# A hybrid decoder layer on one core: the sums of the output weights by accumulating transfers, and the value sums of an attention block in one run

## The chip, the cores and the metric

The kernel runs on one core of a Trainium2 chip. The metric is device time in microseconds of one execution, as the median of several runs. The core has five engines that run side by side, each with an instruction queue worked off in order: TensorE (PE; its weight loads are the row PEld), VectorE (DVE), ScalarE (ACT), GpSimd (POOL) and SyncE (SP), which here only issues transfers. Transfers issued by SP are listed under queue q1, those issued by POOL under q0; both run on the same 16 DMA engines.

## The reference, cut to what matters

One layer is computed for a prompt of 2048 tokens and for 32 sample tokens with a paged cache. A projection `z = rms_norm(x) @ w_in` is split into four groups (convolution, pooling, stick-breaking attention, attention into a memory), each group is gated, and the concatenation goes through `w_out`:

```python
def sb_block(q, k, v, bias, q_pos, k_pos):          # 8 heads of 64, causal
    z = q.k * dh**-0.5 + bias
    log_1m = where(mask, log_sigmoid(-z), 0)
    rc = cumsum(log_1m, reverse=True)               # along the keys
    a = exp(where(mask, log_sigmoid(z) + rc - log_1m, -inf))
    return a @ v
...
mix = concatenate([y_c * silu(cg), y_p * silu(pg), y_s * silu(sg), y_m * silu(mg)])   # 2048 wide
out = rms_norm(mix @ w_out, post_g)                 # w_out: 2048 x 1024
y = rms_norm(x + out, final_g)
```

## The kernel before

The program has three stages. First the input projections, beside them the sample group with its cache, whose pages POOL fetches by indirect transfers (0 to about 1475 us). Then the attention of the prompt (about 1485 to 1922 us). Then the output projection with `w_out`, beside it the end of the convolution group (about 1922 us to the end).

**The attention** (`sb_prompt`) runs over 16 blocks (hp, qb): four pairs of heads, and in each four groups of 512 queries. A block goes over its groups of keys kc from qb down to 0, so qb + 1 of them; over all blocks there are 40 (block, kc) pairs. One such pair is four steps (`score`), one for each head hh of the pair and each half q2 of the queries. A step issues four score products on PE (L1297, L1298: S), on ACT the sigmoids of S (L1302: gam, L1303: be; for some steps DVE forms gam as 1 - be, L1363), two steps later on DVE two scans (L1372 in the diagonal pair, L1375 otherwise: E), and on POOL the multiplication be * E (L1384). Four steps after the score (`TURN`) `turn` puts the 128x128 pieces of be through PE transposes (L1403: AT, two PSUM buffers) and ACT copies them to SBUF (L1405: at, `ATB` buffers). `values` multiplies the turned pieces with V (L1415: av, one PSUM buffer, the two heads side by side in two halves of 64 columns of the array); it is called once for each half q2. When a block's last pair is done, DVE multiplies av by its gate (L1419: sgt, one buffer), SP stores it to `mixd` and then loads the next gate (L1436).

`late` is the list of these delayed calls: each has the step at which it is due, and `behind(step)` issues what is due, after that step's score. A pair that starts at step `base` has its transposes at base + 4, 5, 6 and 7, and its value sums at base + 7 and base + 9.

**Side work** (`side_work`) is a generator, stepped about once for every 4 us of estimated attention time. In this order it runs the end of the sample group, `weight_sums`, the first product's weights (`out_weights(1, ...)`: casts on ACT, low parts on POOL, L1668), the first four operands of the output projection, and the start of `conv_post`.

**The output projection** multiplies 2x2 blocks with seven products instead of eight. Four of them take sums of blocks of `w_out` as weights. `weight_sums` makes those sums: for each of eight row tiles SP loads two tiles of 128x1024 (L1620), POOL forms four differences or sums of 128x512 in SBUF (L1627), and SP stores two tiles to the DRAM tensor `wsd` (L1630). They are read back in the output projection (L1641, L1653). `FACTORS` and `SUMS` say which product uses which.

The order of PE's instructions is the order of the code. On the other engines and on the queues a list scheduler places instructions by its own estimates, within the data dependencies; `tc.issue_after(x)` adds that the instruction stands behind x. Tiles of one tag share the number of buffers given as `bufs`.

Of the kernel before, what the change touches and what calls it, by code (L numbers as in the profile page):

```python
# [18 lines left out]
P = 128  # L19
# [46 lines left out]
SUM = 3  # L66
BEB = 5
ATB = 6
# [24 lines left out]
def kernel(  # L93
# [1227 lines left out]
    def sb_prompt(load, loaded, sb, bps, ops, zmp, early, values_of, flags, newest):  # L1321
# [108 lines left out]
        for bi, (hp, qb) in enumerate(blocks):  # L1430
# [5 lines left out]
            sp.dma_start(gt, gsd[hp, :, 512 * qb : 512 * qb + 512])  # L1436
            carry = {}
            for kc in range(qb, -1, -1):
                base = step
                for q2 in (0, 2):  # L1440
                    for hh in range(2):
                        cost = 1.33 * (2 * q2 + 3) / 4 if kc == qb else 2.66
                        rest = score(hp, qb, kc, hh, q2, Q, KT, carry)
                        if len(pend) == 2:
                            pend.pop(0)()
                        pend.append(rest)
                        yield cost / 2
                        behind(step)
                        step += 1
                        yield cost / 2  # L1450
                for n, q2 in ((0, 0), (2, 2)):
                    late.append((base + n + TURN + SUM, lambda a=(hp, qb, kc, q2, V, gt): values(*a)))
                    for hh in range(2):
                        late.append((base + n + hh + TURN, lambda a=(hp, qb, kc, hh, q2): turn(*a)))
                late.sort(key=lambda x: x[0])
# [9 lines left out]
    def conv_post(cp, ps_, weights):  # L1465
# [61 lines left out]
        def gate(i, co):  # L1527
            a0, a1 = blocks[i]
            gates[i, co] = cp.tile([P, CW], F32, tag="cgt", name=f"cgt{a0}_{co}", bufs=3)
            wq.dma_start(gates[i, co][:, : a1 - a0], gcd[co, :, a0:a1])  # L1530
# [82 lines left out]
    def weight_sums(wsp):  # L1613

        ts = {}
        for j in range(9):
            if j < 8:
                ts[j] = [wsp.tile([P, 2, 512], F32, tag="ws", name=f"ws{j}_{n}", bufs=6) for n in range(2)]
                for t, r in zip(ts[j], half_rows(j)[::-1]):
                    sp.dma_start(t.rearrange("p b n -> p (b n)"), w_out0[r])  # L1620
            yield
            if j:
                t, u = ts.pop(j - 1)
                for o, a, b, op_ in ((t[:, 1], t[:, 1], u[:, 1], ALU.subtract), (u[:, 1], u[:, 1], u[:, 0], ALU.subtract),
                                     (u[:, 0], t[:, 1], u[:, 0], ALU.add), (t[:, 0], t[:, 0], u[:, 0], ALU.subtract)):
                    with tc.issue_after(newest[-1]):
                        pool.tensor_tensor(out=o, in0=a, in1=b, op=op_)  # L1627
                    yield
                for n, o in enumerate((t, u)):
                    sp.dma_start(wsd[n, j - 1], o)  # L1630
                yield

# [103 lines left out]
    def out_combine(x):  # L1736
# [3 lines left out]
        if prod == 5 and i < LAST:  # L1740
            dve.tensor_tensor(out=ts[1], in0=ts[0], in1=ts[1], op=ALU.add)
# [4 lines left out]
        elif prod == 6:  # L1746
            tc.keep_in_program_order(dve.tensor_tensor(out=ts[0], in0=ts[0], in1=ts[1], op=ALU.subtract))
# [25 lines left out]
    def out_ready(prod, i, o):  # L1773

        if i == LAST:
# [12 lines left out]
            else:  # L1788
                dve.tensor_tensor(out=o[:NS], in0=both[:NS], in1=keep["s"][:NS], op=ALU.add)
# [11 lines left out]
        elif prod == 6:  # L1801
            dve.tensor_tensor(out=U3[:, i], in0=o, in1=U3[:, i], op=ALU.add)
            dve.tensor_tensor(out=U2[:, i], in0=o, in1=U2[:, i], op=ALU.add)
# [5 lines left out]
        else:  # L1809
# [9 lines left out]
            dve.tensor_tensor(out=c, in0=o, in1=(U2 if prod == 3 else U3)[:, i], op=ALU.add)  # L1819
# [152 lines left out]
    flags, W, newest = set(), {}, []  # L1972
# [17 lines left out]
    def side_work():  # L1990
# [3 lines left out]
        with tc.tile_pool(name="wsp", bufs=1, side="left", reuse_waits="tile") as wsp:  # L1994
            yield from weight_sums(wsp)
# [217 lines left out]
```

## Time and profile before

| | |
|---|---|
| median of 3 runs | 2313.46 us (2313.35 to 2315.27) |
| the profiled execution | 2319.3 us, of it span of instructions 2317.6 us |
| granted clock of TensorE, mean | 0.993 |
| PE, PEld busy | 2244.9 us (97%), 1812.9 us (78%) |
| DVE, ACT, POOL busy | 1704.7 us (74%), 1081.0 us (47%), 1261.0 us (54%) |
| weight sums (L1627) | 32 instructions on POOL, from 1550.0 to 1762.5 us |
| transfers of the weight sums | 16 loads and 16 stores of 512 KB on SP |

Shares over the whole span are means over three stages that have different limits. What bounds the attention is read from stretches of it: the busy time of each engine in such a stretch, and the granted clock there (1.00 is the upper level of 2.4 GHz, 0.5 is 1.2 GHz). The ends of pipelined matmuls are modelled, so the busy time of PE is read with the distances from start to start in the timeline.

### The profile page before, as it was taken

What the parts mean: (1) busy time and instruction counts of PE and PEld (TensorE: products, weight loads), DVE (VectorE), ACT (ScalarE), POOL (GpSimd) and SP (SyncE); (2) the same over time, 40 slices, a digit from 0 to 9 for tenths busy, and PEclk for the clock granted to TensorE, in tenths of its full rate; (3) what the DMA queues carried; (4) which work ended last, traced back from release to release, by engine and by line L of the source; (5) the groups of instructions that cost most, each with busy time, mean ns of one, the idle gap of its engine ahead of it and who ended that gap; (6) DMA issues with size and microseconds to landing.
All of it is one profiled execution on the core that took longest, in us unless ns stands there. A gap on an engine that the chain in (4) does not pass through costs nothing. (4 is left out here: it accounts for less than half of the span.)

```text
span 2317.6 us, 43407 instructions
## 1 busy us (share of the span) xinstructions
PE 2244.9 (97%) x16512; PEld 1812.9 (78%) x16512; DVE 1704.7 (74%) x2334; ACT 1081.0 (47%) x1977; POOL 1261.0 (54%) x1375
## 2 busy tenths in 40 slices
PE   7999999999999999999999999999999999999997
PEld 7998888898888777777777777667677667788775
DVE  5343786969756755378777768899989885686997
ACT  5332343242442322234233234588879875454553
POOL 3554545556464555555545455489999973620002
PEclk9999999999999999999999999999999999999999
DMA  6689977878778899987977885666554307876774
GB/s 206 208 291 316 336 259 255 286 256 277 255 252 301 306 358 338 345 284 255 319 260 259 278 275 178 160 173 192 160 161 129 98 15 217 285 236 194 251 261 152
DMA packets 338188, 558.32 MB, mean 241 GB/s; under 512 B 29162, under 2 KB 213610, under 8 KB 321580
## 3 DMA queue, kind: packets, MB, share of 16 engines
q1 hardware_dynamic: 282604, 286.83, 39.9%
q0 software_dynamic: 55376, 268.72, 32.8%
q8 instruction: 130, 2.13, 0.4%
q14 instruction: 78, 0.64, 0.1%
HBM read 465.35 MB, written 90.72 MB: 240 GB/s over the span
## 5 line engine op out<-in xcount | busy, mean ns | idle before, releaser
L990 DVE STREAM_TRANSPOSE T<-kt 128x1024 f32<-128x1024 f32 x256 | 308.6, 1226 | 183.1 <-PE sSA L1003 174.8
L957 POOL DMA_INDIRECT vt<-in_cache_v_dram,idv x256 | 252.7, 987 | 255.1 <-PE sO L1042 194.2
L642 DVE SCALAR_TENSOR_TENSOR cacc<-U,par,cacc 128x512 f32<-128x512 f32 x480 | 359.9, 750 | 11.0
L1384 POOL TENSOR_TENSOR be<-be,E 128x512 f32<-128x512 f32 (+4 forms) x316 | 311.9, 999 | 18.0 <-DVE E L1375 12.4
L957 POOL DMA_INDIRECT kt<-in_cache_k_dram,idk x128 | 128.7, 1005 | 200.2 <-DVE T L990 156.0
L1375 DVE TENSOR_TENSOR_SCAN E<-gam,cr,ZM 128x513 f32<-128x513 f32 x192 | 230.6, 1260 | 3.7 <-POOL csq L1499 1.0
L2032 PE MATMUL acc<-wohi,mh 128*128 128x512 f32 (+1 forms) x480 | 192.4, 401 | 0.0
L2032 PE MATMUL acc<-wolo,mh 128*128 128x512 f32 (+1 forms) x480 | 188.7, 393 | 0.0
L2032 PE MATMUL acc<-wohi,ml 128*128 128x512 f32 x448 | 176.9, 395 | 4.7 <-DVE ml L1767 4.7
L1405 ACT COPY at<-AT 128x512 f32<-128x512 f32 (+1 forms) x288 | 153.5, 592 | 47.9 <-PE AT L1403 42.9
L1403 PE MATMUL AT<-ident,be 128*128 128x128 f32 x1082 | 153.3, 281 | 14.6 <-ACT at L1405 10.9
L1403 PEld LDWEIGHTS AT<-ident,be 128*128 128x128 f32 x1082 | 121.2, 143 | 55.0 <-issue 22.8
L1303 ACT ACTIVATE be<-S 128x1024 f32<-128x1024 f32 (+1 forms) x158 | 153.8, 974 | 6.7 <-PE S L1298 4.1
L1415 PE MATMUL av<-at,V 128*64 128x256 f32 (+1 forms) x1152 | 137.4, 379 | 4.2 <-DVE sgt L1419 4.2
L1003 PE MATMUL sSA<-T,W 128*32 128x128 f32 x4096 | 138.3, 276 | 2.0 <-DVE T L990 1.6
L1297 PE MATMUL S<-kh,Q 128*128 128x512 f32 (+1 forms) x316 | 133.4, 426 | 1.5 <-ACT be L1303 1.5
L1003 PEld LDWEIGHTS sSA<-T,W 128*32 128x32 f32 x4096 | 104.6, 109 | 36.9 <-issue 29.0
L1415 PEld LDWEIGHTS av<-at,V 128*64 128x64 f32 x1152 | 76.6, 138 | 61.6 <-issue 23.3
L1042 PE MATMUL sO<-vt,saT 128*32 128x512 f32 x1024 | 122.4, 592 | 0.0
L1298 PE MATMUL S<-kl,Q 66*128 66x512 f32 (+1 forms) x316 | 119.5, 382 | 0.0
L1756 ACT CAST mh<-mr 128x512 fp32r<-128x512 f32 (+1 forms) x120 | 70.5, 596 | 96.5 <-PE acc L2032 26.8
L1767 DVE TENSOR_TENSOR ml<-mr,mh 128x512 fp32r<-128x512 f32 x108 | 80.6, 758 | 40.3 <-ACT mh L1756 40.0
(594 smaller groups left out, 6198.1 us busy)
## 6 DMA issues: line engine op xcount, KB each, us to landing
mr<-mixd SPq DMA_DIRECT2D x32, 512.0 KB
Q<-qd SPq DMA_DIRECT2D x96, 128.0 KB
mr<-mixd SPq DMA_DIRECT2D x48, 256.0 KB
xtp<-in_x_prompt_dram SPq DMA_DIRECT2D x16, 512.0 KB
kh<-kd SPq DMA_DIRECT2D x64, 128.0 KB
ws<-in_w_out_dram SPq DMA_DIRECT2D x16, 512.0 KB
wsd<-ws SPq DMA_DIRECT2D x16, 512.0 KB
msd<-mr SPq DMA_DIRECT2D x32, 256.0 KB
```

The lines of the kernel that those rows point to most:

```text
L642: dve.scalar_tensor_tensor(out=ps, in0=U[:, a + k : a + k + H], scalar=wd[:, k : k + 1], in1=ps, op0=ALU.mult, op1=ALU.add)
L957: pool.indirect_dma_start(out=dst, out_offset=None, in_=rows, in_offset=bass.IndirectOffsetOnAxis(ap=idx, axis=0))
L990: S["turn"] = dve.transpose(T[:, 2 * hh : 2 * hh + 2].rearrange("p s j t -> p (s j t)"), kt[:, 2 * hh : 2 * hh + 2].rearrange("p s j d -> ...
L1003: pe.matmul(sSs[n][32 * g : 32 * g + 32, P * ml : P * (ml + 1)], lhsT=W[:, jj, :], rhs=T[:, :, jj, :], start=i == 0, stop=i == 3, tile_pos ...
L1297: pe.matmul(S[:, j, :w], lhsT=Q[:, 0, c], rhs=kts[0][:, :w], start=True, stop=False)
L1303: act.activation(out=be, in_=S[:, :, :w], func=AF.Sigmoid)
L1375: dve.tensor_tensor_scan(out=E[:, j][:, ::-1], data0=g_[:, j][:, ::-1], data1=ZM[:, 0:1].to_broadcast([P, 513]), initial=carry[hh, q2][:, ...
L1384: newest.append(pool.tensor_tensor(out=be[:, j, :m], in0=be[:, j, :m], in1=E[:, j, 513 - w : 513 - w + m], op=ALU.mult).ins)
L1403: pe.transpose(ap_[:, n : n + P], A[hp, qb, kc, hh, qt][:, P * r : P * (r + 1)], ident)
L1405: act.copy(at[:, :n], ap_[:, :n])
L1415: pe.matmul(av[64 * hh : 64 * hh + 64, c], lhsT=V[:, 4 * kc + r, 64 * hh : 64 * hh + 64], rhs=ats.pop((hp, qb, kc, hh, q2, r)), start=dg a ...
L2032: pe.matmul(o[:rows], lhsT=m[a][:, k, :rows], rhs=W[prod, 4 * h + k][w], start=not cont and h == k == n == 0, stop=h == 1 and k == 3 and n ...
```

## The change

Three things change.

1. `values` of both halves q2 are due at base + 8 (`TURN + SUM` with SUM = 4), so the value sums of a (block, kc) pair stand in one run behind one score, after its last transposes. `at` has eight buffers instead of six.
2. `weight_sums` no longer uses SBUF, POOL arithmetic or the 32 transfers. For each of four sums and each half `a` of the rows SP copies 512x512 values (1 MB) of `w_out` into `wsd` in DRAM, and POOL issues a transfer of 512x512 that is added onto it in DRAM (`accum_op=ALU.add`). There are eight copies and eight accumulating transfers. A copy is issued behind the newest load of a gate (L1436 in the kernel before), one for each new block; the accumulating transfer follows at least one block later. [...]
3. The gate tiles of `conv_post` (cgt) lie in the pool `cpw` instead of `cp`.

```diff
-SUM = 3
+SUM = 4
-ATB = 6
+ATB = 8
...
-            sp.dma_start(gt, gsd[hp, :, 512 * qb : 512 * qb + 512])
+            newest_load.append(sp.dma_start(gt, gsd[hp, :, 512 * qb : 512 * qb + 512]).ins)
...
-                    late.append((base + n + TURN + SUM, lambda a=(hp, qb, kc, q2, V, gt): values(*a)))
+                    late.append((base + TURN + SUM, lambda a=(hp, qb, kc, q2, V, gt): values(*a)))
...
-            gates[i, co] = cp.tile([P, CW], F32, tag="cgt", name=f"cgt{a0}_{co}", bufs=3)
+            gates[i, co] = cpw.tile([P, CW], F32, tag="cgt", name=f"cgt{a0}_{co}", bufs=3)
...
+    def weight_sums():
+        def half(a, h):
+            k = 4 if a == 0 else 0
+            u, t = [w_out0[P * r : P * (r + 4), 512 * h : 512 * h + 512].rearrange("(j p) n -> j p n", p=P)
+                    for r in (8 + 4 * a, k)]
+            return u, t
+        def sums(prod, a):
+            n, h = SUMS[prod]
+            return wsd[n, 4 * a : 4 * a + 4, :, h]
+        def copy(prod, a):
+            u, t = half(a, 0 if prod in (4, 5) else 1)
+            with tc.issue_after(newest_load[-1]):
+                sp.dma_start(sums(prod, a), u if prod == 5 else t)
+        def add(prod, a):
+            of = half(a, 1)[0] if prod in (5, 7) else sums(5 if prod == 6 else 6, a)
+            with tc.issue_after(newest[-1]):
+                pool.dma_start(out=sums(prod, a), in_=of, accum_op=ALU.add)
+        order_ = [(prod, a) for prod in (7, 5, 6, 4) for a in range(2)]
+        seen = len(newest_load)
+        for n in range(9):
+            for _ in range(3):
+                yield
+            if n < 8:
+                while len(newest_load) == seen:
+                    yield
+                seen = len(newest_load)
+                copy(*order_[n])
+            if n:
+                yield
+                add(*order_[n - 1])
...
-            tc.keep_in_program_order(dve.tensor_tensor(out=ts[0], in0=ts[0], in1=ts[1], op=ALU.subtract))
+            tc.keep_in_program_order(dve.tensor_tensor(out=ts[0], in0=ts[0], in1=ts[1], op=ALU.add))
...
-            dve.tensor_tensor(out=U3[:, i], in0=o, in1=U3[:, i], op=ALU.add)
-            dve.tensor_tensor(out=U2[:, i], in0=o, in1=U2[:, i], op=ALU.add)
+            dve.tensor_tensor(out=U3[:, i], in0=U3[:, i], in1=o, op=ALU.subtract)
+            dve.tensor_tensor(out=U2[:, i], in0=o, in1=U2[:, i], op=ALU.subtract)
```

Four other places in `out_combine` and `out_ready` change a sign in the same way; no instruction is added or dropped there.

How the instructions move, at three places. PE before, in the block (hp 2, qb 0), the end of its value sums of the first half and what follows (av2_0 is the sum of that block; S2_1 and AT2_1 belong to the next one):

```order
L1415 MATMUL av2_0_17843<-at2_0_0_1_0_0_17794,V2_17045 64x256
L1415 MATMUL av2_0_17843<-at2_0_0_0_0_0_17763,V2_17045 64x128
L1415 MATMUL av2_0_17843<-at2_0_0_1_0_0_17794,V2_17045 64x128
L1403 MATMUL AT2_0_0_1_2_0_17848<-ident_87,be2_0_0_1_2_17692 128x128 x4
L1403 MATMUL AT2_0_0_1_2_1_17855<-ident_87,be2_0_0_1_2_17692 128x128 x3
L1297 MATMUL S2_1_0_0_0_17861<-kh2_0_0_17023,Q2_1_0_17574 128x512
L1298 MATMUL S2_1_0_0_0_17861<-kl2_0_0_17024,Q2_1_0_17574 128x512
L1297 MATMUL S2_1_0_0_0_17861<-kh2_0_0_17023,Q2_1_0_17574 128x512
L1298 MATMUL S2_1_0_0_0_17861<-kl2_0_0_17024,Q2_1_0_17574 128x512
L1403 MATMUL AT2_1_1_0_0_0_17879<-ident_87,be2_1_1_0_0_17752 128x128 x3
L1297 MATMUL S2_1_0_1_0_17885<-kh2_0_1_17034,Q2_1_1_17585 128x512
```

The value sums of the second half came only after the next step's score, at 7 steps' and 9 steps' distance. PE in the changed kernel, the same block:

```order
L1415 MATMUL av2_0_17818<-at2_0_0_1_0_0_17740,V2_16999 64x256
L1415 MATMUL av2_0_17818<-at2_0_0_0_0_0_17719,V2_16999 64x128
L1415 MATMUL av2_0_17818<-at2_0_0_1_0_0_17740,V2_16999 64x128
L1415 MATMUL av2_0_17818<-at2_0_0_0_2_0_17761,V2_16999 64x256
L1415 MATMUL av2_0_17818<-at2_0_0_1_2_0_17789,V2_16999 64x256
L1415 MATMUL av2_0_17818<-at2_0_0_0_2_0_17761,V2_16999 64x256
L1415 MATMUL av2_0_17818<-at2_0_0_1_2_0_17789,V2_16999 64x256
L1415 MATMUL av2_0_17818<-at2_0_0_0_2_1_17768,V2_16999 64x256
L1415 MATMUL av2_0_17818<-at2_0_0_1_2_1_17796,V2_16999 64x256
L1415 MATMUL av2_0_17818<-at2_0_0_0_2_1_17768,V2_16999 64x128
L1415 MATMUL av2_0_17818<-at2_0_0_1_2_1_17796,V2_16999 64x128
L1403 MATMUL AT2_1_1_0_0_0_17833<-ident_87,be2_1_1_0_0_17690 128x128 x3
```

The second half's sums (at2_0_0_0_2 and at2_0_0_1_2) stand directly behind the first half's, with nothing between them; the transposes follow.

POOL before, around the last pair of keys of block (hp 1, qb 2); ws3 are the two weight tiles of row tile 3:

```order
L1384 TENSOR_TENSOR be1_2_1_1_2_16861<-be1_2_1_1_2_16861,E1_2_1_1_2_16931 128x512
L1627 TENSOR_TENSOR ws3_0_16538<-ws3_0_16538,ws3_1_16539 128x512
L1384 TENSOR_TENSOR be1_2_0_0_0_16898<-be1_2_0_0_0_16898,E1_2_0_0_0_16968 128x512 x2
L1627 TENSOR_TENSOR ws3_1_16539<-ws3_1_16539 128x512
L1384 TENSOR_TENSOR be1_2_0_1_0_16928<-be1_2_0_1_0_16928,E1_2_0_1_0_16996 128x512 x2
L1384 TENSOR_TENSOR be1_2_0_0_2_16966<-be1_2_0_0_2_16966,E1_2_0_0_2_17057 128x512 x2
L1627 TENSOR_TENSOR ws3_1_16539<-ws3_0_16538,ws3_1_16539 128x512
L1384 TENSOR_TENSOR be1_2_0_1_2_16993<-be1_2_0_1_2_16993,E1_2_0_1_2_17086 128x512 x2
```

POOL in the changed kernel, at the same place:

```order
L1384 TENSOR_TENSOR be1_2_1_1_2_16829<-be1_2_1_1_2_16829,E1_2_1_1_2_16903 128x512
L1384 TENSOR_TENSOR be1_2_0_0_0_16857<-be1_2_0_0_0_16857,E1_2_0_0_0_16931 128x512 x2
L1633 DMA wsd_71<-in_w_out_dram 512x512
L1384 TENSOR_TENSOR be1_2_0_1_0_16900<-be1_2_0_1_0_16900,E1_2_0_1_0_16958 128x512 x2
L1384 TENSOR_TENSOR be1_2_0_0_2_16929<-be1_2_0_0_2_16929,E1_2_0_0_2_17011 128x512 x2
L1384 TENSOR_TENSOR be1_2_0_1_2_16955<-be1_2_0_1_2_16955,E1_2_0_1_2_17056 128x512 x2
L1633 DMA wsd_71<-in_w_out_dram 512x512
```

The three sums of that stretch are gone, and the first two accumulating transfers stand there, between the multiplications of the attention. SP before, around the gate of block (hp 2, qb 0):

```order
L1630 DMA wsd_71<-ws5_1_17253 128x1024
L1420 DMA mixd_63<-sgt1_3_17047 128x4x128
L1280 DMA kl3_0_1_18396<-bd_69 2x512
L1290 DMA V3_18406<-vd_59 128x16x128
L1436 DMA sgt2_0_17594<-gsd_61 128x512
L1630 DMA wsd_71<-ws5_0_17252 128x1024
```

SP in the changed kernel, at the same place:

```order
L1420 DMA mixd_63<-sgt1_3_17001 128x4x128
L1276 DMA kh2_3_1_17926<-kd_58 64x512 x2
L1278 DMA kl2_3_1_17927<-kd_58 64x512
L1436 DMA sgt2_0_17532<-gsd_61 128x512
L1628 DMA wsd_71<-in_w_out_dram 512x512
L1420 DMA mixd_63<-sgt2_0_17532 128x4x128
```

The two stores of weight sums, each of which waits for POOL, no longer stand around the store of the block before and the load of the gate; a copy of 1 MB stands behind that load.

## Rows read from the trace of the kernel before

**Rows 1.** Stretches: length; PE, PEld, DVE, ACT, POOL busy; clock, DMA share, GB/s.

```profile
1529.00:1592.00 63.00, 62.70 (x456) 45.98 (x456) 59.25 (x62) 55.62 (x87) 60.17 (x78) 1.00 0.70 198
1592.00:1700.00 108.00, 104.32 (x735) 76.43 (x735) 102.79 (x99) 90.84 (x140) 104.55 (x140) 0.98 0.65 184
1700.00:1766.00 66.00, 63.07 (x432) 46.58 (x432) 59.12 (x63) 54.95 (x85) 63.80 (x91) 0.95 0.42 125
1766.00:1833.00 67.00, 61.90 (x437) 45.59 (x435) 59.56 (x62) 59.46 (x96) 63.85 (x85) 0.97 0.48 132
1833.00:1871.00 38.00, 37.90 (x271) 27.50 (x268) 35.36 (x36) 33.59 (x52) 33.69 (x48) 1.00 0.12 35
...
1922.00:2317.00 395.00, 370.93 (x1776) 304.14 (x1774) 313.48 (x541) 204.12 (x450) 85.02 (x84) 0.99 0.72 232
```

**Rows 2.** PE in order of time, 1647 to 1653 us: start, length, line.

```profile
1648.28 0.40 PE L1297 MATMUL S<-kh,Q 128*128 128x512 f32 x1
1648.51 0.39 PE L1298 MATMUL S<-kl,Q 66*128 66x512 f32 x1
1648.83 1.95 PE L1415 MATMUL av<-at,V 128*64 128x256 f32 x16
1650.71 0.55 PE L1403 MATMUL AT<-ident,be 128*128 128x128 f32 x3
...
1652.34 0.40 PE L1298 MATMUL S<-kl,Q 66*128 66x512 f32 x1
1652.58 0.49 PE L1403 MATMUL AT<-ident,be 128*128 128x128 f32 x3
```

**Rows 3.** PE in order of time, a diagonal run of value sums.

```profile
1598.97 1.73 PE L1415 MATMUL av<-at,V 128*64 128x256 f32 x16
1600.64 0.55 PE L1403 MATMUL AT<-ident,be 128*128 128x128 f32 x3
```

**Rows 4.** Groups by line, 1529 to 1766 us: busy, mean ns, idle before and releasers.

```profile
L1363 DVE TENSOR_SCALAR gam<-be 128x1024 f32<-128x1024 f32 x32 | 37.3, 1164 | 10.7 <-ACT be L1303 10.7
L1627 POOL TENSOR_TENSOR ws<-ws,ws 128x512 f32<-128x512 f32 x24 | 32.6, 1357 | 0.0
...
L1627 POOL TENSOR_TENSOR ws<-ws 128x512 f32<-128x512 f32 x8 | 10.8, 1345 | 0.0
```

**Rows 5.** PE in order of time, 1624 to 1632 us, two idle times in brackets.

```profile
1627.53 0.33 PE L1403 MATMUL AT<-ident,be 128*128 128x128 f32 x1 [1.12 <-POOL be L1384]
1628.70 0.98 PE L1403 MATMUL AT<-ident,be 128*128 128x128 f32 x7 [0.85 <-POOL be L1384]
```

**Rows 6.** SP's queue in order of time, 1695 to 1725 us: start and length of the issue.

```profile
1697.59 0.61 SPq L1278 DMA_DIRECT2D kl<-kd  x1
1703.01 0.34 SPq L1630 DMA_DIRECT2D wsd<-ws  x1
1703.46 0.39 SPq L1420 DMA_DIRECT2D mixd<-sgt  x1
...
1707.12 0.47 SPq L1436 DMA_DIRECT2D sgt<-gsd  x1
```

**Rows 7.** DVE and PE in order of time, where that gate is used.

```profile
1712.04 0.69 DVE L1419 TENSOR_TENSOR sgt<-av,sgt 128x512 f32<-128x512 f32 x1 [1.65 <-DMA sgt<-gsd]
...
1712.78 1.55 PE L1415 MATMUL av<-at,V 128*64 128x256 f32 x8 [2.83 <-DVE sgt L1419]
```

**Rows 8.** Waits, 1485 to 1922 us: us in total, times, longest.

```profile
PE AT L1403 <- ACT at L1405: 9.6, 12, 3.0
```

**Rows 9.** The instructions on `mixd`: one transfer that POOL issues, and its landing.

```profile
L1420 POOL DMA_DIRECT2D mixd<-sgt x1: 879/879/879, 1922.6 to 1922.6; - x1
...
DMA to landing us min/median/max: 6.1/6.1/6.1
```

**Rows 10.** DVE in order of time: the end of three blocks.

```profile
1658.58 0.66 DVE L1419 TENSOR_TENSOR sgt<-av,sgt 128x512 f32<-128x512 f32 x1
...
1763.01 0.67 DVE L1419 TENSOR_TENSOR sgt<-av,sgt 128x512 f32<-128x512 f32 x1
...
1870.44 0.66 DVE L1419 TENSOR_TENSOR sgt<-av,sgt 128x512 f32<-128x512 f32 x1
```

**Rows 11.** SP and POOL in order of time, in block (hp 2, qb 3).

```profile
1769.44 0.33 SPq L1436 DMA_DIRECT2D sgt<-gsd  x1
...
1777.86 1.09 POOL L1384 TENSOR_TENSOR be<-be,E 128x512 f32<-128x512 f32 x1
```

More of the change, by code (lines that the diff above doesn't have):

```diff
@@ L1611 @@
     SUMS = {4: (0, 0), 7: (0, 1), 6: (1, 0), 5: (1, 1)}
[L1613 to L1627, printed above, removed]
+    def weight_sums():
[22 more added lines that the diff above has]
+                while len(newest_load) == seen:
                     yield
-                for n, o in enumerate((t, u)):
-                    sp.dma_start(wsd[n, j - 1], o)
+                seen = len(newest_load)
+                copy(*order_[n])
+            if n:
                 yield
+                add(*order_[n - 1])
     def weight_load(prod, j, raw):
@@ L1740, in out_combine @@
         if prod == 5 and i < LAST:
-            dve.tensor_tensor(out=ts[1], in0=ts[0], in1=ts[1], op=ALU.add)
+            dve.tensor_tensor(out=ts[1], in0=ts[1], in1=ts[0], op=ALU.subtract)
             ts = ts[1:]
@@ L1788, in out_ready @@
             else:
-                dve.tensor_tensor(out=o[:NS], in0=both[:NS], in1=keep["s"][:NS], op=ALU.add)
+                dve.tensor_tensor(out=o[:NS], in0=both[:NS], in1=keep["s"][:NS], op=ALU.subtract)
                 square(o, 16, 1)
@@ L1818, in out_ready @@
                     g[0] = op.tile([P, 2, 512], F32, tag="raw", name=f"og{t}_0", bufs=RAWS)[:, 0]
-            dve.tensor_tensor(out=c, in0=o, in1=(U2 if prod == 3 else U3)[:, i], op=ALU.add)
+            dve.tensor_tensor(out=c, in0=o, in1=(U2 if prod == 3 else U3)[:, i],
+                              op=ALU.subtract if prod == 5 else ALU.add)
             square(c, t, half)
@@ L1971 @@
     seconds, shared = {}, {}
-    flags, W, newest = set(), {}, []
+    flags, W, newest, newest_load = set(), {}, [], []
     def side_ps(name):
@@ L1993, in side_work @@
             yield from sample_end(sm2, side_ps, S)
-        with tc.tile_pool(name="wsp", bufs=1, side="left", reuse_waits="tile") as wsp:
-            yield from weight_sums(wsp)
+        yield from weight_sums()
         opm = ox.enter_context(tc.tile_pool(name="opm", bufs=1, side="left", reuse_waits="tile"))
```

## The prediction

> **What bounds the kernel now.** I read the table of the span in slices first, to see which stage the change touches, then the attention by stretches, then PE's timeline inside it, and last the waits. The change touches the attention (1485 to 1922 us) and, by its sums and signs, the output projection. In the stretches [rows 1] the reader is to see that in the attention no engine is far from full: between 1529 and 1766 us, where the weight sums run, PE is busy for 62.70 + 104.32 + 63.07 = 230.1 of 237 us (97%), POOL for 228.5 (96%), DVE for 221.2 (93%), ACT for 201.4 (85%). Shares this close don't say who bounds. PE's own timeline does: in undisturbed stretches the next matmul starts right behind the last one (1529 to 1592 us: 0.3 us idle; 1833 to 1871 us: 0.1 us idle), while DVE is idle for 3.7 and 2.6 us there. So PE is the bound wherever nothing disturbs it, with DVE and POOL a few per cent behind, and POOL's backlog is what disturbs it. What PE loses to disturbances can be added up: idle time, plus the share of the stretch that the granted clock was below 1.00. From 1529 to 1766 us it is 6.9 us idle and 0.02 x 108 + 0.05 x 66 = 5.5 us of clock, 12.4 us in all; from 1766 to 1833 us, where no weight sum runs any more, 5.1 + 0.03 x 67 = 7.1 us; from 1833 to 1871 us 0.1 us.
>
> **One run of value sums instead of two (term 1).** A score matmul starts 0.23 us after the one before it (1648.28 to 1648.51), a transpose 0.24 us after a score matmul (1652.34 to 1652.58), but a run of value sums 0.32 us after one (1648.51 to 1648.83): 0.09 us to enter [rows 2]. The run of 16 records (eight pairs, the two heads side by side) takes 1.88 us up to the next transpose [rows 2]; a diagonal run, in which two of the eight pairs are half as wide, takes 1.67 us (1598.97 to 1600.64) [rows 3]. So one pair costs 0.21 us, eight cost 1.7, and about 0.2 us goes into starting and ending the run. Each run costs 0.25 to 0.29 us beyond its work; I take 0.25. There are 80 runs, two for each of 40 (block, pair of key groups); the order of the changed kernel shows them joined without anything between. 40 x 0.25 = 10.0 us less on PE. This counts in full where PE is the bound and not at all where POOL or DVE is, so its bounds are 0 and 11.6 us.
>
> **Weight sums off POOL (term 2).** Removed are 24 x 1357 + 8 x 1345 ns = 43.4 us of POOL [rows 4]. Added are eight transfers that POOL issues. The trace has one plain transfer issued by POOL, also of 512 pieces: 879 ns [rows 9]. It is neither accumulating nor from DRAM to DRAM, so I bound the new one from below by nothing and from above by the price at which all is given back, 43.4 / 8 = 5.4 us; I take the row, 8 x 0.88 = 7.0 us. POOL then has 228.5 - 43.4 + 7.0 = 192.1 of 237 us, 81%, and is no longer near the bound. What PE gets back is worth counting place by place. At 1627 to 1629 us PE waits twice for POOL's multiplication, 1.12 + 0.85 us [rows 5], and the clock of that stretch loses 2.2 us: 4.1 us. At 1712 us PE waits 2.83 us for DVE, which has waited 1.65 us for the gate [rows 7]. The gate's load is late because SP is held by a store of weight sums that waits for POOL: nothing is issued between 1697.59 and 1703.01 us, and the store of the block before and then the load (1707.12) come behind it [rows 6]. In the changed order no store that waits for POOL stands there. That is 2.83 us and 3.3 us of clock, 6.1 us. Together 10.2 us of the 12.4 have a cause that goes. I take 10. The bounds are 0 (the stalls come back with another cause) and 12.4 + 7.1 = 19.5 us (the backlog also made those after 1766 us).
>
> **What is late next (term 3).** A joined run keeps PE away from scores and transposes for 3.5 us instead of 1.9. ACT stands in order and waits behind it for transposes, then delivers its copies late. In the trace PE waits 9.6 us for those copies in 12 waits [rows 8], over 80 runs. Half as many runs, each twice as long, could leave that or double it: between 0 and 9.6 us more. I take 7, near the upper end, since ACT with 85% has little idle time in which to catch up. The eight at buffers are just those of one run, and the run stands ahead of the next transposes in PE's order, so no transpose waits for a buffer; six would not do. The value sums of the next block now start four steps after those of the last instead of two, so PE waits less for DVE to empty av; that is inside term 2.
>
> **What costs nothing.** The sign changes keep instruction and shape. Of the copies (8 x 1 MB on SP) and the accumulating transfers nobody reads the result before the output projection, except an accumulating transfer itself (a rival, below). The DMA engines are busy 42 to 70% in that stretch [rows 1]. The copies stand behind the gate's load, and ahead of the next gate's store, which has a block's time. The casts of the first product's weights come one place later beside POOL's and ACT's work. In the output projection the scheduler shuffles ACT and DVE somewhat; PE is busy 370.9 of 395 us there [rows 1], and I take 0 with 3 us either way. Moving cgt to another pool changes no instruction: 0.
>
> **Sum.** -10.0 - 10 + 7 = -13 us. Against the profiled execution (2319.3 us, 1.7 us of it outside the span) that is 2306.3. The profile lies 5.8 us above the median of 2313.46; the same difference from the median gives 2300.5 us.
>
> **Rivals.**
>
> *PE takes all (2284 us).* Terms 1 and 2 at their upper ends and nothing for term 3: 10 + 19.5 = 29.5 us less. For it: the stretch from 1833 us shows PE without a gap at 89% POOL. Against it: DVE is busy 93% in the same stretch, and from 1766 to 1833 us POOL has its own 95% with weights' low parts that stay.
>
> *The sums were hidden (2312 us).* The sharpest evidence against my term 2: from the end of one block (1658.58) to the end of the block four later (1763.01) the kernel needs 104.4 us with weight sums, and for the same four kinds of blocks after them (1763.01 to 1870.44) 107.4 us [rows 10]. By that POOL's relief is worth nothing, DVE and ACT hold the pace, and the 10 us of term 1 are eaten by term 3 at its upper end, 9.6, with 1 us gained. Against it: in the second set POOL still has eight low parts and four operands, and the 7.1 us lost from 1766 to 1833 us lie in it; without these it would be 100.3.
>
> *POOL is stopped by the accumulating transfer (2320 us, slower).* It must wait for the copy that it adds to, and behind it in POOL's order stand the multiplications of the attention, for which PE's transposes wait. Of the eight, two stand close behind their copy: the last one at what is now 1777.86 us, 8.4 us behind its gate's load at 1769.44 [rows 11], the fifth about 10 us behind. Nothing in the trace shows 1 MB from DRAM to DRAM. 256 KB took 4.9 us (the load at 1707.12, used at 1712.04) [rows 6, 7] and 6.1 us [rows 9]. So 1 MB lands after 6 us, if most of that is fixed, or 20 us, if all of it grows with the size; I take 9, near the lower end, as in that stretch the DMA engines are half idle. At 20 us POOL stops for 11 + 10 us, and PE loses that and some clock, less what the buffers hold: about 20 us against the 13 gained, so 7 us slower. It decides from a landing of about 16 us. The Trainium skill (DMA: Bandwidth & Descriptors, Anatomy of one DMA) gives a transfer issued by GpSimd as about 2.0 us plus its bytes at 436 GB/s: by it, as an estimate, 1 MB lands in 4.4 us, and this rival would have no chance at all. The trace doesn't bear that out at this size, since the same formula has 2.6 us for the 256 KB that took 4.9 and 6.1.
>
> **How the numbers follow.** I give the forecast, about -7 to -20 us, half of the chance; PE takes all 0.12; the sums were hidden 0.20; POOL is stopped 0.10; 0.08 is for the shuffled order of the output projection either way. What a measurement of this kernel can tell from no change is 0.2%, 4.6 us: 2308.8 to 2318.1 us. Faster are the forecast, the first rival, a little of the second and half of the rest: 0.72. Slower are the third rival and a little of the rest: 0.11. The same: 0.17. The range runs from 2289 us, which leaves out most of the first rival, to 2313 us, which takes in the hidden sums and leaves out the stopped POOL. The forecast's own range is 2293 to 2307 us.
>
> **What would show it.** Right: 40 runs of 32 records of L1415 that take about 3.5 us; POOL below 85% between 1529 and 1766 us; no wait of PE for the gate around 1712 us; the last L1419 about 13 us earlier and the projection behind it as long as before. Wrong: POOL issues of more than 2 us, or a gap on POOL ahead of L1633; PE waiting for ACT's copies for more than 20 us in all; four blocks from end to end that still take 104 us [rows 10] with POOL at 80%.

## The result, and the profile after

The changed kernel takes 2331.03 us (median of 12 runs, 2325.34 to 2335.57), the kernel before 2320.38 us in the same comparison (2313.35 to 2327.43). The ratio is 1.0046, 95% interval 1.0033 to 1.0058: slower by 10.7 us, where 2300.5 was forecast and 2313 was the end of the range. Part of the distance is the level that the forecast started from, 2313.46 us as the median of three runs; from 2320.38 its -13 us would lead to 2307.4, still some 24 us below the measured time. The profiled execution has a span of 2331.1 us, 13.5 more than before.

The stretches of the attention in the trace after, with the columns of [rows 1]; the last is from the last gate multiplication to the end:

```profile
1529.00:1592.00 63.00, 56.79 (x405) 43.15 (x404) 53.55 (x51) 51.20 (x77) 48.58 (x65) 0.97 0.54 140
1592.00:1700.00 108.00, 97.23 (x678) 72.26 (x675) 88.64 (x94) 84.44 (x131) 81.28 (x119) 0.97 0.60 138
1700.00:1766.00 66.00, 63.81 (x468) 47.68 (x466) 60.81 (x65) 55.89 (x90) 56.56 (x80) 1.00 0.83 197
1766.00:1833.00 67.00, 63.95 (x460) 48.11 (x458) 59.03 (x63) 58.70 (x93) 60.07 (x87) 1.00 0.67 156
...
1939.50:2331.00 391.50, 372.64 (x1786) 308.78 (x1786) 312.43 (x541) 204.39 (x451) 80.25 (x84) 0.98 0.72 235
```

From 1529 to 1766 us POOL is busy for 186.4 of 237 us (79%), as forecast, but PE too has sunk, from 230.1 [rows 1] to 217.8 us, and in the first two stretches it executes 108 matmuls fewer than before. An engine that had been let go would show more work in the same time. In the first two stretches all engines sink together: they wait for each other. From the last gate multiplication to the end it is 391.6 us, against 396.0 before, so the attention itself ends 17.9 us later (before, then after):

```profile
1921.57 0.69 DVE L1419 TENSOR_TENSOR sgt<-av,sgt 128x512 f32<-128x512 f32 x1 [2.80 <-PE av L1415]
```
```profile
1939.47 0.69 DVE L1419 TENSOR_TENSOR sgt<-av,sgt 128x512 f32<-128x512 f32 x1 [2.50 <-PE av L1415]
```

The parts of the change by themselves look as forecast. A joined run (PE in order of time) and the groups of the accumulating transfers (line, count: shortest, median, longest in ns; below them from issue to landing):

```profile
1741.16 3.67 PE L1415 MATMUL av<-at,V 128*64 128x256 f32 x32
```
```profile
L1633 POOL DMA_DIRECT2D wsd<-in_w_out_dram x4: 1035/1118/1412, 1645.5 to 1710.3; - x4
...
L1633 POOL DMA_DIRECT2D wsd<-wsd x4: 1012/1026/1221, 1734.5 to 1795.8; - x4
...
DMA to landing us min/median/max: 9.9/11.7/15.3
```

The run takes 3.61 us to the next transpose (1744.77), against 2 x 1.88 in two pieces [rows 2]. The issue costs POOL 1.0 to 1.4 us, and the trace shows no wait of POOL ahead of these transfers. The gate of the block that stopped PE for 2.83 us before [rows 7] comes in time:

```profile
1728.22 0.67 DVE L1419 TENSOR_TENSOR sgt<-av,sgt 128x512 f32<-128x512 f32 x1
```

Where the time went shows in the ends of blocks. First the ends of two blocks and of those ahead of them in the kernel before:

```profile
1521.96 0.67 DVE L1419 TENSOR_TENSOR sgt<-av,sgt 128x512 f32<-128x512 f32 x1
...
1550.98 0.67 DVE L1419 TENSOR_TENSOR sgt<-av,sgt 128x512 f32<-128x512 f32 x1
...
1602.90 0.67 DVE L1419 TENSOR_TENSOR sgt<-av,sgt 128x512 f32<-128x512 f32 x1
...
1621.90 0.67 DVE L1419 TENSOR_TENSOR sgt<-av,sgt 128x512 f32<-128x512 f32 x1
```

Then the changed kernel, with what stopped POOL, DVE and PE in these two (start, length, in brackets the idle time before and what ended it):

```profile
1545.76 0.73 POOL L1483 TENSOR_TENSOR cs<-cy 128x256 f32<-128x256 f32 x1 [6.41 <-DMA cy<-ydw]
```
```profile
1523.26 0.67 DVE L1419 TENSOR_TENSOR sgt<-av,sgt 128x512 f32<-128x512 f32 x1
...
1559.88 0.66 DVE L1419 TENSOR_TENSOR sgt<-av,sgt 128x512 f32<-128x512 f32 x1
...
1614.04 0.67 DVE L1419 TENSOR_TENSOR sgt<-av,sgt 128x512 f32<-128x512 f32 x1
...
1637.21 7.15 DVE L1375 TENSOR_TENSOR_SCAN E<-gam,cr,ZM 128x513 f32<-128x513 f32 x6
1644.28 0.66 DVE L1419 TENSOR_TENSOR sgt<-av,sgt 128x512 f32<-128x512 f32 x1
...
1672.31 0.69 DVE L1419 TENSOR_TENSOR sgt<-av,sgt 128x512 f32<-128x512 f32 x1 [2.50 <-PE av L1415]
...
1778.99 0.66 DVE L1419 TENSOR_TENSOR sgt<-av,sgt 128x512 f32<-128x512 f32 x1
...
1888.81 0.67 DVE L1419 TENSOR_TENSOR sgt<-av,sgt 128x512 f32<-128x512 f32 x1
```
```profile
1645.00 4.54 PE L1415 MATMUL av<-at,V 128*64 128x256 f32 x24 [6.36 <-DVE sgt L1419]
```

Block (hp 0, qb 2), 1523.26 to 1559.88, takes 36.6 us instead of 29.0: the first addition of the convolution's totals (L1483) stands in POOL's queue ahead of the block's last multiplications, and waits 6.41 us for its load. Block (hp 1, qb 1), 1614.04 to 1644.28, takes 30.2 instead of 19.0: eight more scans and a complement gate now stand on DVE ahead of the gate multiplication, six of the scans in the row above, and until it has emptied av, PE's next run waits 6.36 us. The four blocks from 1672.31 to 1778.99 take 106.7 us and the next four 109.8, against 104.4 and 107.4 [rows 10]; neither of these two stalls stands in these, and they are 2.3 and 2.4 us slower.

Both stalls are a matter of order, and the order of the changed kernel shows them before any run. DVE there, in the order of its queue, around that gate multiplication (before, it stands directly behind the scans of E1_2_1_0_0, so nine instructions earlier):

```
L1375 SCALAR_TENSOR_TENSOR E1_2_1_0_0_16804<-gam0_14901,cr1_2_2_0_0_16684,ZM_14899 128x513 x2
L1375 SCALAR_TENSOR_TENSOR E1_2_1_1_0_16832<-gam1_14903,cr1_2_2_1_0_16714,ZM_14899 128x513 x2
L1363 TENSOR_SCALAR gam2_14905<-be1_2_1_0_2_16802 128x2x512
L1375 SCALAR_TENSOR_TENSOR E1_2_1_0_2_16860<-gam2_14905,cr1_2_2_0_2_16745,ZM_14899 128x513 x2
L1375 SCALAR_TENSOR_TENSOR E1_2_1_1_2_16903<-gam0_14901,cr1_2_2_1_2_16787,ZM_14899 128x513 x2
L1375 SCALAR_TENSOR_TENSOR E1_2_0_0_0_16931<-gam1_14903,cr1_2_1_0_0_16807,ZM_14899 128x513 x2
L1419 TENSOR_TENSOR sgt1_1_16349<-av1_1_16619,sgt1_1_16349 128x512
```

Beside them stands the wait of [rows 8], which has doubled (us in total, times, longest, over the attention):

```profile
PE AT L1403 <- ACT at L1405: 20.4, 29, 1.6
```

### The profile page after: what moved, and what is told of

Same layout as the page of the kernel before. It is cut to its first block, busy times and chain, and to the rows that moved or that the text cites. A ratio compares the mean times of both kernels' runs of the same rounds, so it can differ in the third digit from the quotient of the medians.

```text
span 2331.1 us, 43257 instructions
## 1 busy us (share of the span) xinstructions
PE 2247.8 (96%) x16512; PEld 1826.7 (78%) x16512; DVE 1698.8 (73%) x2334; ACT 1078.8 (46%) x1977; POOL 1226.8 (53%) x1351
## 5 line engine op out<-in xcount | busy, mean ns | idle before, releaser
L1375 DVE TENSOR_TENSOR_SCAN E<-gam,cr,ZM 128x513 f32<-128x513 f32 x192 | 230.4, 1260 | 15.7 <-ACT gam L1302 10.1
L1403 PE MATMUL AT<-ident,be 128*128 128x128 f32 x1082 | 154.9, 281 | 24.8 <-ACT at L1405 20.4
L1003 PEld LDWEIGHTS sSA<-T,W 128*32 128x32 f32 x4096 | 104.5, 109 | 36.7 <-issue 29.1
L1415 PEld LDWEIGHTS av<-at,V 128*64 128x64 f32 x1152 | 86.0, 141 | 53.7 <-issue 9.4
L1372 DVE TENSOR_TENSOR_SCAN E<-gam,ZM 128x384 f32<-128x384 f32 (+1 forms) x124 | 94.6, 811 | 15.3 <-POOL be L1384 5.9
```

Source lines behind the costliest of these rows:

```text
L1003: pe.matmul(sSs[n][32 * g : 32 * g + 32, P * ml : P * (ml + 1)], lhsT=W[:, jj, :], rhs=T[:, :, jj, :], start=i == 0, stop=i == 3, tile_pos ...
L1375: dve.tensor_tensor_scan(out=E[:, j][:, ::-1], data0=g_[:, j][:, ::-1], data1=ZM[:, 0:1].to_broadcast([P, 513]), initial=carry[hh, q2][:, ...
L1403: pe.transpose(ap_[:, n : n + P], A[hp, qb, kc, hh, qt][:, P * r : P * (r + 1)], ident)
L1415: pe.matmul(av[64 * hh : 64 * hh + 64, c], lhsT=V[:, 4 * kc + r, 64 * hh : 64 * hh + 64], rhs=ats.pop((hp, qb, kc, hh, q2, r)), start=dg a ...
```

## The experiments

A key group is one (block, kc) pair. Theory A: the joined run makes ACT's copies late and so gives back what it saves; the rest of the loss is the two badly placed instructions; the weight sums by transfers cost nothing. Theory B: the transfers and what they move cost the time. Each run was compared with the kernel before in the same series; its median was 2317.5 to 2320.8 us there.

**The sums alone, and the run alone.**

```diff
-SUM = 4                       # sums_only, from the changed kernel
+SUM = 3
-ATB = 8
+ATB = 6
-late.append((base + TURN + SUM, lambda ...
+late.append((base + n + TURN + SUM, lambda ...
```

`run_only` is the opposite edit on the kernel before, with cgt in cpw for room; `sums_only` has cgt there too, as the changed kernel has.

> The changed kernel with the value sums of a key group split in two runs again and six turned buffers: the weight sums by accumulating transfers alone. Theory A (the joined run makes the copies on ScalarE late, and two instructions that the scheduler now places badly, the conv totals on GpSimd and a gate multiplication on VectorE, stall once each): not slower than before, 2308 to 2320 us, 0.995 to 1.000 of before; a stall at the conv totals or at the gate of the second block of a pair shows as 3 to 8 us in that block. Theory B (the accumulating transfers and what they move cost the time): 2326 us or more, 1.0025 or more of before.

> The kernel before with the value sums of a key group in one run and eight turned buffers (and the gate tiles of the convolution in the later pool, for room): the weight sums stay GpSimd's. Theory A: slower than before, 2322 to 2332 us, 1.001 to 1.005, with TensorE waiting for ScalarE's copies of turned tiles for over 15 us in the attention (9.6 before), and each off-diagonal key group of the last head pair 0.3 to 0.6 us longer. Theory B: 2306 to 2318 us, 0.994 to 0.999, the ten microseconds of TensorE that the forecast counted less what GpSimd hides.

Measured: `sums_only` 2317.84 us, 0.9995 (0.9984 to 1.0005); `run_only` 2318.53 us, 1.0000 (0.9985 to 1.0015). `sums_only` is as theory A has it. Both stalls are in it, too: the gate multiplication of block (hp 1, qb 1) is seven instructions late instead of nine, and PE waits 5.9 us for it; the totals wait 1.41 us for their load.

```profile
PE av L1415 <- DVE sgt L1419: 7.6, 4, 5.9
```
```profile
1544.83 0.73 POOL L1483 TENSOR_TENSOR cs<-cy 128x256 f32<-128x256 f32 x1 [1.41 <-DMA cy<-ydw]
```

`run_only` has neither wait. It is faster than theory A expected and slower than theory B expected. Its busy times over the attention show both halves of the account, before and then with the joined run, and its waits:

```profile
1485.00:1925.00 440.00, 420.98 (x2942) 308.21 (x2942) 389.80 (x396) 364.96 (x568) 393.65 (x529) 0.98 0.47 132
```
```profile
1485.00:1925.00 440.00, 412.89 (x2929) 311.34 (x2929) 393.96 (x395) 363.20 (x568) 393.38 (x529) 0.99 0.45 130
```
```profile
PE AT L1403 <- ACT at L1405: 19.3, 29, 1.7
```

PE needs 8.1 us less for 13 matmuls fewer (term 1 said 10; against `cgt_only`, below, which differs by the run alone, it is 6.4), and waits 9.7 us more for ACT's copies than in [rows 8]. Neither part alone, each with cgt moved, makes the kernel slower than before; the loss comes from the two together.

**The two instructions held.**

```diff
+                    with tc.issue_after(newest[-1]):          # cs_held
                         pool.tensor_tensor(out=sums[i], ...
...
+                gated.append((count["rest"], dve.tensor_tensor(out=gt, in0=av, ...).ins))   # both_held, too
+                old = [g for n, g in gated if count["rest"] - n > 2]
+                with tc.issue_after(old[-1]) if old else ExitStack():
                     ... the scans of a step
```

> The changed kernel with the three additions of the conv totals issued behind the attention products that stand ahead of them in program order, so that they no longer stand ahead of their load on GpSimd in the third block. Theory A: 5 to 8 us off the changed kernel, 2323 to 2326 us, and that block 29 to 30 us instead of 36.6. Theory B: within 2 us of the changed kernel, since that block is then held by the next late thing.

> The changed kernel with the conv totals held as above and with the scans of VectorE held behind the gate multiplication of the block before from the third pair on, which puts the gate multiplications of the second head pair's blocks where the kernel before has them. Theory A: both one-off stalls go, 8 to 13 us off the changed kernel, 2318 to 2323 us, 0.999 to 1.001 of before, with the 0.5 us per off-diagonal key group left. Theory B: within 3 us of the changed kernel.

Measured: `cs_held` 2324.69 us, 1.0026 (1.0014 to 1.0038); `both_held` 2315.82 us, 0.9983 (0.9972 to 0.9994). Block (hp 0, qb 2) of `cs_held` and block (hp 1, qb 1) of `both_held`:

```profile
1531.13 0.67 DVE L1419 TENSOR_TENSOR sgt<-av,sgt 128x512 f32<-128x512 f32 x1
...
1561.94 0.67 DVE L1419 TENSOR_TENSOR sgt<-av,sgt 128x512 f32<-128x512 f32 x1
```
```profile
1606.73 0.67 DVE L1422 TENSOR_TENSOR sgt<-av,sgt 128x512 f32<-128x512 f32 x1
...
1629.49 0.68 DVE L1422 TENSOR_TENSOR sgt<-av,sgt 128x512 f32<-128x512 f32 x1
```

30.8 us instead of 36.6, and 22.8 instead of 30.2. `cs_held` is within theory A's range; `both_held` is faster than theory A's 2318 us and 0.999, so the hold of the scans gave more than expected. From the ratios the totals cost 0.0020 (4.6 us of 2320) and the gate 0.0043 (10.0 us). Together they are more than the whole loss. For the transfers themselves theory B falls, since the same transfers run in `both_held`. What their edit moved in the order of the others does cost time.

**The sums alone, held.**

```diff
-SUM = 4                       # from both_held
+SUM = 3
-ATB = 8
+ATB = 6
-late.append((base + TURN + SUM, lambda ...
+late.append((base + n + TURN + SUM, lambda ...
```

> The changed kernel with two runs of value sums per key group and six turned buffers, as in the kernel before, and with the conv totals and the scans of VectorE held as in the last experiment: the weight sums by accumulating transfers alone, without the two badly placed instructions. Theory A (TensorE is the bound of the attention, so GpSimd's 43 us were hidden, and what the transfers give is the two waits at gates that go): 2308 to 2317 us, 0.995 to 0.999 of before, the attention up to the last gate multiplication no more than 8 us shorter than before. Rival (GpSimd's relief was worth the ten microseconds of the forecast): 2305 to 2309 us, 0.9935 to 0.995.

Measured: 2311.09 us, 0.9961 (0.9947 to 0.9975): theory A, with an interval that reaches into the rival's. Against `sums_only` (0.9995), which differs by the two holds alone, it gains 0.0034, 7.9 us. With all else in the code equal, the joined run costs 0.9983 - 0.9961 = 0.0022, 5.1 us. Block (hp 1, qb 2) takes 29.5 us, and the four blocks behind the end of it 101.2 us, where before took 36.7 and 104.4:

```profile
1622.31 0.68 DVE L1422 TENSOR_TENSOR sgt<-av,sgt 128x512 f32<-128x512 f32 x1
...
1651.84 0.67 DVE L1422 TENSOR_TENSOR sgt<-av,sgt 128x512 f32<-128x512 f32 x1
...
1753.02 0.66 DVE L1422 TENSOR_TENSOR sgt<-av,sgt 128x512 f32<-128x512 f32 x1
```

From 1529 to 1766 us (columns of [rows 1]) PE now executes 54 matmuls more than the 1619 of before, at full clock:

```profile
1529.00:1766.00 237.00, 233.38 (x1673) 171.56 (x1672) 217.99 (x227) 208.87 (x322) 200.55 (x287) 1.00 0.71 170
```

Part of it is lost again in block (hp 2, qb 3), 49.0 us instead of 42.0, where ACT waits for weights whose load stands behind the last head pair's keys on SP:

```profile
1794.49 0.62 ACT L1683 CAST wohi<-wor 128x512 fp32r<-128x512 f32 x1 [5.08 <-DMA wor<-in_w_out_dram]
```

**That load two tiles ahead.**

```diff
-        yield from out_weights(1, opm, pool)
+        yield from out_weights(1, opm, pool, 2)
```

> The kernel with the sums by transfers alone and both instructions held (labelled sums_held), with the output weights of the first product loaded two tiles ahead of their cast instead of one, since the cast of the fourth waited 5.1 us on ScalarE for a load that stands behind the last head pair's keys on SyncE's queue. If that wait is what made the last block of the third head pair 49.0 us where before has 42.0: that block 42 to 45 us and 2305 to 2309 us, 0.9935 to 0.996. If it is covered: as sums_held, 0.996 to 0.997.

Measured: 2310.07 us, 0.9957 (0.9943 to 0.9971). The block takes 43.3 us as expected, but the last one 55.3 instead of 52.3, and the total, 1 us above the expected range, is not to be told from `sums_held`. Either beats both kernels, the one before and the changed one.

**The run behind the next transposes.** On `both_held`:

```diff
-            while late and late[0][0] <= limit:
+            while late and int(late[0][0]) <= limit:
...
-late.append((base + TURN + SUM, lambda ...
+late.append((base + TURN + SUM + 0.5, lambda ...
```

> The last kernel with both instructions held and the joined run, with the run put behind the first transposes of the next key group instead of ahead of them, so that ScalarE has two copies to make while the run is on TensorE; still eight turned buffers, so these copies wait for the run's first matmuls. Theory A (the joined run's ten microseconds are given back as waits of TensorE for ScalarE's copies): the 20 us of waits for copies fall to 12 or less and the time to 2304 to 2313 us, 0.993 to 0.997 of before. Rival (ScalarE as a whole, not the place of the run, limits a key group): the waits for copies are named at another line but stay at 17 us or more, 2313 to 2320 us, 0.997 to 1.000.

Measured: 2347.53 us, 1.0118 (1.0093 to 1.0144): worse than either expectation, and PE's waits for copies did not fall to 12 us but rose to 47.3. ACT now has copies to make during the run (6.6 us of waits of them are for buffers that the run has to free), but the next scores come only behind it. ACT's waits for scores, 8.6 us in `both_held`, become 78.5 us:

```profile
ACT gam L1302 <- PE S L1298: 78.5, 37, 3.3
```
```profile
1784.68 1.03 ACT L1302 ACTIVATE gam<-S 128x1024 f32<-128x1024 f32 x1 [2.74 <-PE S L1298]
```

In both orders ACT runs out of work during a run of 3.6 us: of transposes in the one, of scores in the other.

**Less work for ACT.** One more of the four complement gates of an off-diagonal key group (DVE forms one already) is taken off ACT, first on `both_held` (`run_...`), then on `sums_lead` (`sums_...`).

```diff
-            rest_of = q2 == 2 and (dg or hh == 0)
+            rest_of = q2 == 2 and (dg or hh == 0) or not dg and (hh, q2) == (1, 0)     # run_dve_gate, sums_dve_gate
...
+            by_pool = not dg and (hh, q2) == (1, 0)                                    # run_pool_gate, sums_pool_gate
...
+                    (pool if by_pool else dve).tensor_scalar(out=ga, ...
```

> The kernel with the joined run and both instructions held (labelled both_held), with one of the four complement gates of an off-diagonal key group (line 1302, 0.92 us on ScalarE) computed by GpSimd from the finished gate instead, 24 in all. Theory A (in a group of the joined run ScalarE, with some 10.5 us of work, idles while the run of 3.6 us holds TensorE, and the group of 12.06 us is ScalarE's work and that idle time): ScalarE's 22 us less shorten the off-diagonal groups of the last three head pairs by 0.3 to 0.7 us each, waits of TensorE for copies fall from 20 to under 13 us, 2302 to 2310 us, 0.993 to 0.997 of before. Rival (the copies wait for the place in ScalarE's order, not for its load, or GpSimd, given 24 x 1.7 us, is late in turn): 0.997 to 1.002.

> The kernel labelled sums_lead with the same 24 complement gates on GpSimd. Theory A (with two shorter runs TensorE, not ScalarE, is the bound): no gain on sums_lead, within 0.1%, or a loss of up to 0.3% by GpSimd. Rival (ScalarE's copies limit the split runs too): 0.15 to 0.5% less than sums_lead.

Measured: 2337.24 us, 1.0076 (1.0059 to 1.0094), and 2344.93 us, 1.0104 (1.0082 to 1.0127). Both are slower than any of their expectations, and neither tells the theories apart, since the edit puts a new wait into the path. DVE's scans wait for POOL in `run_pool_gate`:

```profile
DVE E L1379 <- POOL gam L1364: 56.9, 22, 5.7
```

So the same was given to DVE, which stands before the scan in any case.

> The kernel labelled both_held with one of the four complement gates of an off-diagonal key group (24 in all, 0.92 us each on ScalarE) computed by VectorE from the finished gate (line 1363, 0.73 us), so that nothing new stands between GpSimd and the scans, which was what spoilt the try with GpSimd. Theory A (in a group of the joined run ScalarE's work and its idle time during the run make the 12.06 us): TensorE's waits for copies fall from 20 to under 14 us, 2303 to 2311 us, 0.9935 to 0.997 of before. Rival (VectorE, with 86 of 94 us busy, becomes the bound, or only the order counts): 0.998 to 1.005.

> The kernel labelled sums_lead with the same 24 complement gates on VectorE. Theory A (with two shorter runs ScalarE keeps up and TensorE is the bound): within 0.15% of sums_lead, 0.994 to 0.997 of before, or slower by VectorE. Rival (ScalarE limits the split runs as well): 0.991 to 0.994.

Measured: `run_dve_gate` 2309.89 us, 0.9966 (0.9950 to 0.9981), where `both_held` had 0.9983; `sums_dve_gate` 2318.17 us, 1.0008 (0.9992 to 1.0024), where `sums_lead` had 0.9957. The split kernel's loss of 0.0051 is clear of the intervals; the joined kernel's gain of 0.0017 is not, by time alone. Its waits show more. PE's waits for the copies in `both_held` and in `run_dve_gate`, 12.1 us where theory A had under 14:

```profile
PE AT L1406 <- ACT at L1408: 20.1, 28, 2.1
```
```profile
PE AT L1406 <- ACT at L1408: 12.1, 12, 3.2
```

In the split kernels they rise, from 10.1 to 15.0 us. The start of the value sums in two key groups one behind the other, block (hp 1, qb 3): joined (`both_held`), joined with less work for ACT (`run_dve_gate`):

```profile
1674.48 3.67 PE L1418 MATMUL av<-at,V 128*64 128x256 f32 x32
1682.73 1.06 PE L1406 MATMUL AT<-ident,be 128*128 128x128 f32 x8 [0.79 <-ACT at L1408]
1686.10 3.67 PE L1418 MATMUL av<-at,V 128*64 128x256 f32 x32
```
```profile
1668.31 3.67 PE L1418 MATMUL av<-at,V 128*64 128x256 f32 x32
1679.08 3.67 PE L1418 MATMUL av<-at,V 128*64 128x256 f32 x32
```

Between the two starts PE does the same work in both kernels. It takes 11.62 us joined and 10.77 with ACT relieved, and 0.79 of the 0.85 us between them is the wait for the copy. The same pair of groups gives the same in the first head pair (11.62 and 10.78); in the last two, where side work stands beside it, the relieved kernel is the longer one (12.74 against 12.24, 13.60 against 11.19), so the mechanism is seen in half of these places. ACT during the joined run of 1674.48:

```profile
1676.44 1.12 ACT L1303 ACTIVATE be<-S 128x1024 f32<-128x1024 f32 x1
1678.78 1.08 ACT L1408 COPY at<-AT 128x512 f32<-128x512 f32 x2 [1.21 <-PE AT L1406]
1680.17 1.03 ACT L1302 ACTIVATE gam<-S 128x1024 f32<-128x1024 f32 x1 [0.32 <-PE S L1298]
```

ACT idles 1.21 us until the transposes come behind the run, and PE, which then needs 1.9 us for a step (0.83 for the transposes, 1.1 for the scores) where ACT needs 2.8 (0.92 + 0.92 for two sigmoids, 2 x 0.48 for the copies), gets ahead, until both AT buffers are full. More AT or S buffers, which would be another way to give ACT work for the length of the run, were not tried.

**The edit that was to cost nothing.** On the kernel before:

```diff
-            gates[i, co] = cp.tile([P, CW], F32, tag="cgt", ...
+            gates[i, co] = cpw.tile([P, CW], F32, tag="cgt", ...
```

> The kernel before with the gate tiles of the convolution in the later pool and nothing else. All the changed variants take 389 to 393 us from the last gate multiplication to the end where before takes 396. If this edit, which the forecast put at nothing, is the cause: 392 to 393 us behind the last gate multiplication and 0.998 to 0.999 of before. If it is the output projection's other order or the scatter of one execution: 0.9995 to 1.0005.

Measured: 2315.66 us, 0.9981 (0.9964 to 0.9998), and 392.1 us behind the last gate multiplication. PE's waits for DVE's ml there, before and then with cgt moved:

```profile
PE acc L2032 <- DVE ml L1767: 4.7, 5, 1.2
```
```profile
PE acc L2032 <- DVE ml L1767: 1.5, 2, 1.1
```

So it is this edit rather than the sums that goes with the shorter output projection, by some 4 us. Its interval nearly reaches 1, and the medians of the two kernels in that series (2315.66 and 2317.82 us) lie only 2.2 us apart; but the profiles of all thirteen kernels with the edit have 389 to 393 us there, against 396.0 in the one profile of before. Why another pool changes these waits is not shown.

## Why the prediction was wrong, point by point

The difference of 10.7 us can be split along a chain of kernels, `cgt_only`, `sums_held`, `both_held`, `cs_held` and the changed one (differences of ratios, times 2320 us; by their intervals each is uncertain by 4 to 5 us, so that only the gate stands far clear of noise, the weight sums not at all, and the other three just): cgt -4.4; the weight sums by transfers -4.6 (`sums_held` less `cgt_only`); the joined run +5.1 (`run_only` less `cgt_only`, without the transfers, gives +4.4); the gate multiplication +10.0 (the hold acts on all blocks; block (hp 1, qb 1) has some 7 us of it); the totals +4.6. In a chain the parts add up to the whole by themselves, so the sum proves nothing.

- **The step that failed is "what costs nothing"**: the forecast looked at the order only where the text of the change pointed, at value sums, weight sums and stores, and took the reshuffling elsewhere as 0 with 3 us either way, in the output projection alone. The order of DVE and POOL in the attention held two misplaced instructions, the gate multiplication of block (hp 1, qb 1) and the totals of the convolution, which cost 14.6 us. They could have been read before the run: for each instruction that stands elsewhere than before, ask what it waits for and what stands behind it. "Moving cgt to another pool changes no instruction: 0" failed, too, in the other direction (-4.4). Nothing here speaks against the 0 for the signs: three sums are kept with the opposite sign, because the transfers are issued with `accum_op=ALU.add`, and no instruction came of it.
- **Term 1** was right as PE's busy time: 6.4 to 8.1 us measured, 10 forecast.
- **Term 3** was the right mechanism with the wrong size. It took 7 us, so that a joined run still gained 3; PE's waits for copies rose by 9.7 to 10.8 us, just beyond its upper bound of 9.6, and the run cost 5.1 us net. The forecast argued from ACT's share of 85%; what the runs show is a price per key group: a run longer than ACT's stock of work, followed by steps faster than ACT's.
- **Term 2** was right at its places and too large in its net: POOL fell to 79%, the stalls at 1627 us and at the gate at 1712 us went, and block (hp 1, qb 2) fell from 36.7 to 29.5 us in `sums_held`. But of 10 us only 4.6 came through, if that. By the trace of `sums_held`, counted from the first gate multiplication, 8.3 us were gained by the end of block (hp 2, qb 2), and 7.0 were given back in the next block, at the cast; in `sums_lead` 8.4 us were gained by the end of block (hp 3, qb 2), and 4.1 given back in the last.
- **The rivals.** "The sums were hidden" came nearest by its size: a small gain for the sums and the run's gain eaten by the copies. Its test, four blocks that still take 104 us with POOL at 80%, came out in the changed kernel (106.7), but there the joined run lengthens them too; with the split run of `sums_held` the four take 101.2 us, so the sums were not wholly hidden. "POOL is stopped" did not occur: POOL shows no wait ahead of L1633. When the copies land, the trace doesn't say. The accumulating transfers landed 9.9 to 15.3 us after their issue. By the Trainium skill (DMA: Bandwidth & Descriptors, Anatomy of one DMA) 1 MB takes, as an estimate, 4.4 us; the transfers measured here took two to three and a half times that, beside other traffic, so the measurement decides.
- **The signs of being wrong** named one that came: PE's waits for copies of more than 20 us in all (20.4). The one that carried the loss, an instruction of another part placed late, was not among them.

What stays open: why the scheduler places the two instructions so. The kernel with the joined run alone has neither stall, the one with the transfers alone has both, with shorter waits (5.9 and 1.41 us instead of 6.36 and 6.41). So the misplacing comes with the edit of the weight sums, and the joined run adds to it; how the scheduler's estimates come to that, these runs don't show. Nor do they show what the last block loses in `sums_lead`, or why `sums_dve_gate` is slower than it.

## What to carry to other kernels

Where a scheduler places instructions, compare the order of every engine over the whole stage, not only at the lines of the edit: one multiplication nine instructions late cost twice what the run's joining did. Joining short runs on the engine that looks like the bound pays only if the engine that feeds on it has work for the length of the run; test that by taking work off that engine, and look whether the waits for it go and not only at the total. And time a change's parts one by one with the order held, since here a gain of 9 us lay in a kernel that was 10.7 us slower.

## What the runs showed of the hardware

A transfer of 1 MB that is added from DRAM onto DRAM, issued by GpSimd, occupied GpSimd for 1.0 to 1.4 us and landed 9.9 to 15.3 us after its issue, with the DMA engines 60 to 83% busy. In `run_pool_gate` a `tensor_scalar` of 128x1024 took GpSimd 1.05 us where VectorE took 0.70 (medians); VectorE's scans waited 2.6 us at a time for it (56.9 / 22), so longer than it lasts: part of the wait is for its turn in GpSimd's queue.
